# A hybrid diffusion-transformer layer on one core: the mixing projection's sums and operand splits go from GpSimd to VectorE, six of its weight blocks are split ahead, and a third early block's weights get tiles of their own

## The chip, the cores and the metric

One NeuronCore of a Trainium2 chip runs the whole layer in one launch. The metric is the device time in microseconds (us). The kernel before was timed three times: 2280.68, 2282.3 and 2285.83 us, median 2282.3. One execution was also recorded by the hardware profiler. TensorE is called PE in the profile (PEld is its weight load), VectorE is DVE, ScalarE is ACT, GpSimd is POOL, and SyncE is SP, whose queue issues every transfer here.

## The reference, cut to what matters

```python
mix = merge_branches(...)                 # ends in: return merged @ w_o
x_new = x + g1 * mix                      # 1024 tokens x 1024 channels
h2 = modulate(rmsnorm(x_new, norm2_g), sh2, sc2)   # * sc2 + sh2 per channel
x_new = x_new + g2 * swiglu(h2, w_ffn_in, w_ffn_out)

def swiglu(h, w_in, w_out):
    gu = h @ w_in                         # (1024, 1024) @ (1024, 5632)
    return (jax.nn.silu(gu[..., :D_FF]) * gu[..., D_FF:]) @ w_out
```

The change concerns the stretch from `merged @ w_o` to the first columns of `h @ w_in`.

## The kernel before, in words

All matrix products are made of three products of 128x512 outputs: an fp32 operand is split into a high part (`hi`, rounded by ScalarE to the type the PE reads) and a low part (`lo`, the fp32 value minus `hi`), and hi·hi, hi·lo and lo·hi are summed in PSUM (`mm3`, L203 to L205). So each operand block costs a cast on ScalarE and a subtraction on VectorE or GpSimd before the PE can use it.

Three stages touch the change. The stage ahead (the SSD output projection) ends with the gated sums `m1`, which are split into `mg[k][hf]` (L1229 to L1234). Beside it VectorE builds the second half of the adaLN vectors (L1194, L1196), and weights come through a pool of two raw tiles and three hi and lo tiles of 1024 columns each, filled by `wload` and `wsplit` (L198, L199).

The mixing projection (from L1271) goes over two halves `dh` of the output's columns. For each it needs eight weight blocks of 128x512, `wo[k]`. In the first half, blocks 0 to 2 come through that pool, each in one half of a 1024-column tile; blocks 3 to 7, and all eight of the second half, come through a pool `pe` that opens only with this stage: two raw tiles `wor`, nine tiles each of `woh` and `wol`, the low part on GpSimd (L1291). Then eight token blocks `t` follow: 24 matmuls into `em`, times the gate `g1bc` on VectorE (L1302), plus the residual `xr` (L1303, on GpSimd in the second half except for t = 7), a store to `s_xn`, and a sum of squares on ScalarE (L1305). In the second half VectorE and GpSimd make 1/rms (L1310 to L1312), VectorE scales (L1314), the PE transposes (L1317), and VectorE and ScalarE write the modulated `h2` in turn (L1324, L1321), four pieces of 128x128 for each group of transposes.

The feed-forward's input projection works with 2x2 blocks in seven products instead of eight (a Strassen scheme): its right-hand operands are quadrants of `h2` and their sums. `opB11` and `opB21` are the first two quadrants, complete after t = 3; they are split on ScalarE and GpSimd (`msplit(..., 1)`, L1263, L1264). Each of 22 steps `j` has two products that need only these (`f_first`), of 12 matmuls each, and five that need the rest. `f_first` for j = 0, 1 and 2 is placed ahead of the rest (L1372, L1374, L1400), so that the PE has work while the last token blocks are normalised. The weight block of j = 2 is the fourth in a ring `fraw` of three tiles, and the first tile of that ring is free when `w_combos(0)` has read it (L1407 to L1410 on VectorE). The other operands follow: `opB22` (L1264 again), `opT3`, `opT1`, `opT2` (`tsplit`, L1383, L1384, in a pool `mp2` of 24 tiles of 128x512) and `opT4`. Weight operands are split by `opsplit` (L1343, L1344); its argument `e` picks GpSimd (1) or VectorE (0) for the low part. In the first eleven steps each step also forms sums of output weights for the later stage (loads `fi`, sums on VectorE in L1437, stores `s_cw`).

The order on every engine is fixed when the kernel is built: a scheduler places the instructions of this part by its own cost model, and each engine then works through its list in order. A waiting instruction holds up everything behind it on its engine; SP's list does the same to transfers. Tiles of a pool that opens later lie where tiles of closed pools lay, and their first writer waits for the last reader of that memory, tile by tile.

Of the kernel before, what the change touches and what calls it, by code (L numbers as in the profile page):

```python
# [15 lines left out]
P = 128  # L16
# [125 lines left out]
def _build(nc, tc, h, o, hook, stop, es):  # L142
# [47 lines left out]
    def wload(src, cols=1024):  # L190
        raw = wp.tile([P, 1024], F32, name="wraw", bufs=NRAW)
        nc.sync.dma_start(out=raw[:, :cols], in_=src)
        return wsplit(raw, cols)
# [1074 lines left out]
    with pool("pe", "left") as pe, pool("ppe", "left", space=PSUM) as ppe:  # L1268
# [3 lines left out]
        for dh in range(2):  # L1272
# [8 lines left out]
            for k in range(KT):  # L1281
                if dh == 0 and k < NHL:
                    hi, lo = wload(h["wo"][k][:, ds_], 512)
                    wo.append((hi[:, :512], lo[:, :512]))
                    continue
                raw = pe.tile([P, 512], F32, name="wor", bufs=2)
                nc.sync.dma_start(out=raw, in_=h["wo"][k][:, ds_])
                hi = pe.tile([P, 512], F32R, name="woh", bufs=9)
                lo = pe.tile([P, 512], F32R, name="wol", bufs=9)
                nc.scalar.copy(out=hi, in_=raw)  # L1290
                nc.gpsimd.tensor_tensor(out=lo, in0=raw, in1=hi.bitcast(F32), op=ALU.subtract)  # L1291
                wo.append((hi, lo))
            for t in range(NT):
# [8 lines left out]
                nc.vector.tensor_tensor(out=x_, in0=ps, in1=g1bc[:, ds_], op=ALU.mult)  # L1302
                (nc.gpsimd if dh == 1 and t < NT - 1 else nc.vector).tensor_tensor(out=x_, in0=x_, in1=xr, op=ALU.add)  # L1303
                nc.sync.dma_start(out=s_xn[t][:, ds_], in_=x_)
# [8 lines left out]
                for q in range(2):  # L1313
# [4 lines left out]
                    for i in range(4):  # L1318
                        k = 4 * q + i
                        if i % 2:  # L1320
                            nc.scalar.activation(out=h2[hf][:, k, ts_], in_=tp[:, i, :], func=AF.Identity,  # L1321
                                                 scale=sc2[:, k:k + 1], bias=sh2[:, k:k + 1])
                        else:
                            nc.vector.tensor_scalar(out=h2[hf][:, k, ts_], in0=tp[:, i, :], scalar1=sc2[:, k:k + 1],  # L1324
                                                    scalar2=sh2[:, k:k + 1], op0=ALU.mult, op1=ALU.add)
                if t == 3:
                    for i in range(4):
                        opB11[i] = msplit(h2[0][:, i, :], 1)
                        opB21[i] = msplit(h2[0][:, 4 + i, :], 1)
                        nc.gpsimd.tensor_tensor(out=h2[0][:, 4 + i, :], in0=h2[0][:, 4 + i, :], in1=h2[0][:, i, :], op=ALU.subtract)  # L1330
# [33 lines left out]

    def f_first(j, pss=None, e=1):
        if (j, 0) not in fw:
            f_load(j, 0)
        rg = fw[(j, 0)]
        f12[j] = pss or [fq_ps() for _ in range(2)]
        product(f12[j][0], opsplit(rg[:, :512], e), opB11)  # L1370
        product(f12[j][1], opsplit(rg[:, 512:], 0), opB21)

    f_load(0, 0)
    f_load(0, 1)  # L1374
    f_first(0)
    ppf = es.enter_context(pool("ppf", "left", space=PSUM))
    f_first(1, [fq_ps(), fp_ps()])
    mp2 = fstack.enter_context(pool("mp2", "left"))

    def tsplit(src):  # L1380
# [17 lines left out]

    f_hold(1)
    f_first(2, [fp_ps(), fp_ps()])  # L1400
    f_hold(2)

# [13 lines left out]
    for i in range(4):  # L1416
        opB22[i] = msplit(qd(i)[3])
    product(p3_0, opsplit(wc[0][3], 1), opB22)
    for i in range(4):
# [12 lines left out]
    with pool("fb", "right") as fb, pool("fg", "right") as fg:  # L1432
# [25 lines left out]
        for j in range(NFF):  # L1458
# [13 lines left out]
            product(p7, opsplit(s3, 0), opT3)  # L1472
            product(p5, opsplit(s1, 1), opT1)
            product(p6, opsplit(w2, 0), opT2)
# [185 lines left out]
```

## Time and profile before

| | |
|---|---|
| median of three runs | 2282.3 us |
| profiled execution, device time | 2281.2 us |
| its span, first to last instruction | 2279.4 us |
| mean granted TensorE clock | 0.981 of full |
| PE busy | 2165.9 us (95%) |
| DVE busy | 1627.0 us (71%) |
| ACT busy | 991.4 us (43%) |
| POOL busy | 741.8 us (33%) |

The profiled execution lies 1.1 us under the median, and 1.8 us of it lie outside the span. Busy shares are means over stages with different limits; in this kernel the PE is busy nearly throughout, so the time that can go is where the PE stands still or runs at its lower clock. Times within the span are counted from its start. In the views of single instructions a row gives start, duration, engine, line, operation, output and inputs, count, and in brackets how long the engine stood idle before it and what ended that.

### The profile page before, as it was taken

Reading aid. Unit: us, or ns where it says so; the run is one execution under the profiler, and the core shown is the slowest. Engines: PE = TensorE matmul, PEld = TensorE weight load, DVE = VectorE, ACT = ScalarE, POOL = GpSimd, SP = SyncE. Lnnn points to the kernel's source line nnn. Section 1 sums busy time; section 2 is a strip of 40 time slices with the busy share of each in tenths; the row PEclk is TensorE's granted clock in tenths of the full one; section 3 lists DMA queues with packets and bytes.
Section 4 is the critical chain, followed back from the end, with each engine's and each line's share of the span. In section 5 each row is a group of like instructions: output and inputs, shape, how many; then the busy total and the mean of one; then the engine's idle time right before and its main releaser. Section 6 shows DMA issues by size and latency. Waiting matters only on the chain. (4 is left out here: it accounts for less than half of the span.)

```text
span 2279.4 us, 32757 instructions
## 1 busy us (share of the span) xinstructions
PE 2165.9 (95%) x11560; PEld 1813.0 (80%) x11560; DVE 1627.0 (71%) x2783; ACT 991.4 (43%) x2094; POOL 741.8 (33%) x610
## 2 busy tenths in 40 slices
PE   7999999999689999999999999999798999999997
PEld 1778888886588999999989887777576888887876
DVE  5878888888657777877736558826987566775678
ACT  4444444433345666767743212124422332334443
POOL 1532111110125555555521222135343333332222
PEclk9999999999799999999999999999899999999999
DMA  8122223432254555555454546551486224457755
GB/s 289 64 73 88 83 84 130 143 119 93 90 171 152 176 160 171 173 175 178 156 188 164 177 159 245 186 187 65 127 276 226 92 98 162 166 177 242 237 194 185
DMA packets 167101, 360.28 MB, mean 158 GB/s; under 512 B 17548, under 2 KB 57228, under 8 KB 166296
## 3 DMA queue, kind: packets, MB, share of 16 engines
q1 hardware_dynamic: 166936, 358.18, 47.0%
q8 instruction: 91, 1.49, 0.3%
q14 instruction: 74, 0.61, 0.1%
HBM read 267.34 MB, written 90.78 MB: 157 GB/s over the span
## 5 line engine op out<-in xcount | busy, mean ns | idle before, releaser
L199 POOL TENSOR_TENSOR wlo<-wraw,whi 128x1024 fp32r<-128x1024 f32 (+1 forms) x83 | 201.5, 2431 | 634.3 <-ACT whi L198 631.5
L198 ACT CAST whi<-wraw 128x1024 fp32r<-128x1024 f32 (+1 forms) x123 | 126.8, 1036 | 237.6 <-PE dm L210 84.2
L203 PE MATMUL fill<-whi,hhi 128*128 128x256 f32 x768 | 223.1, 292 | 7.1 <-DVE pad L576 5.8
L432 DVE SCALAR_TENSOR_TENSOR cv<-pad,vecs,cv 128x1282 f32<-128x1282 f32 (+1 forms) x128 | 213.8, 1709 | 7.8 <-ACT cv L429 7.4
L204 PE MATMUL fill<-wlo,hhi 128*128 128x256 f32 x768 | 218.1, 284 | 0.0
L205 PE MATMUL fill<-whi,hlo 128*128 128x256 f32 x768 | 217.4, 284 | 0.0
L874 ACT ACTIVATE abc<-abc,a_all 128x128 f32<-128x128 f32 x512 | 158.2, 392 | 88.4 <-DMA abc<-s_a 84.1
L203 PE MATMUL fp<-m,oph 128*128 128x512 f32 x452 | 181.3, 402 | 14.0 <-ACT oph L1343 10.4
L205 PE MATMUL fp<-m,opl 128*128 128x512 f32 x452 | 181.7, 403 | 8.0 <-DVE opl L1344 5.0
L204 PE MATMUL fp<-m,oph 128*128 128x512 f32 x452 | 181.2, 401 | 0.0
L495 PE MATMUL mm<-tq,whi 128*128 128x512 f32 x480 | 153.8, 401 | 1.4 <-ACT whi L198 1.4
L203 PEld LDWEIGHTS fill<-whi,hhi 128*128 128x128 f32 x768 | 145.8, 190 | 9.4 <-issue 6.2
L495 PE MATMUL mm<-hhi,whi 128*128 128x512 f32 x320 | 127.7, 400 | 22.4 <-DVE pad L570 22.4
L204 PEld LDWEIGHTS fill<-wlo,hhi 128*128 128x128 f32 x768 | 146.3, 191 | 0.7
L205 PEld LDWEIGHTS fill<-whi,hlo 128*128 128x128 f32 x768 | 146.0, 190 | 0.5
L495 PE MATMUL mm<-hlo,whi 128*128 128x512 f32 x320 | 127.1, 397 | 0.0
L495 PE MATMUL mm<-hhi,wlo 128*128 128x512 f32 x320 | 126.9, 397 | 0.0
L203 PEld LDWEIGHTS fp<-m,oph 128*128 128x128 f32 x452 | 86.5, 191 | 36.1 <-ACT oph L1343 11.7
L205 PEld LDWEIGHTS fp<-m,opl 128*128 128x128 f32 x452 | 86.3, 191 | 32.0 <-DVE opl L1344 7.6
L495 PEld LDWEIGHTS mm<-tq,whi 128*128 128x128 f32 x480 | 89.7, 189 | 22.7 <-ACT whi L198 2.5
L850 DVE SCALAR_TENSOR_TENSOR S<-S,decp,st 128x64 f32<-128x64 f32 x512 | 105.0, 273 | 0.0
L876 DVE COPY_PREDICATED abc<-misc,abc 128x512 f32<-128x512 int32 x64 | 52.3, 818 | 71.2 <-ACT abc L874 71.1
(408 smaller groups left out, 5919.0 us busy)
## 6 DMA issues: line engine op xcount, KB each, us to landing
abc<-s_a SPq DMA_DIRECT2D x64, 512.0 KB
fraw<-in_wfi SPq DMA_DIRECT2D x44, 512.0 KB
wraw<-in_wxbc SPq DMA_DIRECT2D x32, 512.0 KB
dx<-in_wada SPq DMA_DIRECT2D x32, 512.0 KB
wraw<-in_wzf SPq DMA_DIRECT2D x24, 512.0 KB
gt<-s_gate SPq DMA_DIRECT2D x24, 512.0 KB
fi<-in_wfo SPq DMA_DIRECT2D x22, 512.0 KB
s_cw<-fo SPq DMA_DIRECT2D x44, 256.0 KB
```

The lines of the kernel that those rows point to most:

```text
L198: nc.scalar.copy(out=hi[:, :cols], in_=raw[:, :cols])
L199: (eng or nc.gpsimd).tensor_tensor(out=lo[:, :cols], in0=raw[:, :cols], in1=hi[:, :cols].bitcast(F32), op=ALU.subtract)
L203: nc.tensor.matmul(ps, lhsT=a[0], rhs=b[0], start=start, stop=False)
L204: nc.tensor.matmul(ps, lhsT=a[0], rhs=b[1], start=False, stop=False)
L205: nc.tensor.matmul(ps, lhsT=a[1], rhs=b[0], start=False, stop=stop)
L432: nc.vector.scalar_tensor_tensor(out=v[:, :n], in0=pd[:, t:t + n], scalar=cwh[:, 5 * b + t:5 * b + t + 1], in1=v[:, :n], op0=ALU.mult, op1 ...
L495: nc.tensor.matmul(ps, lhsT=lhs[x], rhs=b[i][y], start=i == 0 and (x, y) == (0, 0), stop=i == 3 and (x, y) == (1, 0))
L850: nc.vector.scalar_tensor_tensor(out=sn[:, hd_], in0=S[-1][:, hd_], scalar=decp[:, i, d, 4 * g + j:4 * g + j + 1], in1=sv_[:, hd_], op0=AL ...
L874: nc.scalar.activation(out=abc[:, d, j, :], in_=abc[:, d, j, :], func=AF.Identity, scale=-1.0, bias=a_all[:, c, hd:hd + 1])
L876: nc.vector.copy_predicated(out=E, mask=tri_b.bitcast(mybir.dt.int32)[:, None, :].to_broadcast([P, HPG, P]), data=abc[:, 1])
```

## The change

In the first half of the projection six of the eight weight blocks now come through the older pool, two in each 1024-column tile (two transfers of 256 KB, one cast, one subtraction), and that subtraction is on VectorE. The low parts of the other two are on VectorE too. The residual additions of the second half are all on VectorE. For t below 7 ScalarE writes three of four pieces of `h2`, VectorE one. The low parts of `opB11` and `opB21`, those of the first products of j = 0, 1 and 2, and of two more weight operands of j = 0, are on VectorE. The weight block of j = 2 no longer waits for the ring: it is loaded into two of the 24 tiles of `mp2`.

```diff
-                if dh == 0 and k < NHL:
-                    hi, lo = wload(h["wo"][k][:, ds_], 512)
-                    wo.append((hi[:, :512], lo[:, :512]))
+                if dh == 0 and k < 2 * NHL:
+                    if k % 2 == 0:
+                        raw = wp.tile([P, 1024], F32, name="wraw", bufs=NRAW)
+                        for q in range(2):
+                            nc.sync.dma_start(out=raw[:, 512 * q:512 * q + 512], in_=h["wo"][k + q][:, ds_])
+                        hi, lo = wsplit(raw, eng=nc.vector)
+                        wo += [(hi[:, :512], lo[:, :512]), (hi[:, 512:], lo[:, 512:])]
                     continue
...
-                nc.gpsimd.tensor_tensor(out=lo, in0=raw, in1=hi.bitcast(F32), op=ALU.subtract)
+                (nc.gpsimd if dh else nc.vector).tensor_tensor(out=lo, in0=raw, in1=hi.bitcast(F32), op=ALU.subtract)
...
-                (nc.gpsimd if dh == 1 and t < NT - 1 else nc.vector).tensor_tensor(out=x_, in0=x_, in1=xr, op=ALU.add)
+                nc.vector.tensor_tensor(out=x_, in0=x_, in1=xr, op=ALU.add)
...
-                        if i % 2:
+                        if i % 2 or (i and t < NT - 1):
...
-                        opB11[i] = msplit(h2[0][:, i, :], 1)
-                        opB21[i] = msplit(h2[0][:, 4 + i, :], 1)
+                        opB11[i] = msplit(h2[0][:, i, :])
+                        opB21[i] = msplit(h2[0][:, 4 + i, :])
...
-    def f_first(j, pss=None, e=1):
-        if (j, 0) not in fw:
+    def f_first(j, pss=None, e=1, raw=None):
+        if (j, 0) not in fw and raw is None:
             f_load(j, 0)
-        rg = fw[(j, 0)]
+        rg = fw.get((j, 0))
         f12[j] = pss or [fq_ps() for _ in range(2)]
-        product(f12[j][0], opsplit(rg[:, :512], e), opB11)
-        product(f12[j][1], opsplit(rg[:, 512:], 0), opB21)
+        rg = (rg[:, :512], rg[:, 512:]) if raw is None else raw
+        product(f12[j][0], opsplit(rg[0], e), opB11)
+        product(f12[j][1], opsplit(rg[1], 0), opB21)
...
-    f_first(0)
+    f_first(0, e=0)
...
-    f_first(1, [fq_ps(), fp_ps()])
+    f_first(1, [fq_ps(), fp_ps()], e=0)
     mp2 = fstack.enter_context(pool("mp2", "left"))
+    early = [mp2.tile([P, 512], F32, name="m2", tag="m2", bufs=24) for _ in range(2)]
+    for q in range(2):
+        nc.sync.dma_start(out=early[q], in_=h["wfi"][2][:, 512 * q:512 * q + 512])
...
-    f_first(2, [fp_ps(), fp_ps()])
+    f_first(2, [fp_ps(), fp_ps()], e=0, raw=early)
...
-    product(p3_0, opsplit(wc[0][3], 1), opB22)
+    product(p3_0, opsplit(wc[0][3], 0), opB22)
...
-            product(p5, opsplit(s1, 1), opT1)
+            product(p5, opsplit(s1, int(j > 1)), opT1)
```

The built order shows what this moves. First the PE at the start of the mixing projection, before: the first matmuls that need a block of the later pool (`woh`, `wol`), behind 27 that need only blocks split ahead (`whi`, `wlo`; `m` is `mg`, `em_15072`, `em_15104` and `em_15136` are t = 0, 1 and 2).

```order
L205 MATMUL em_15136<-whi_15038,m_14544 128x512
L203 MATMUL em_15072<-woh_15044,m_14646 128x512
L203 MATMUL em_15104<-woh_15044,m_14646 128x512
L203 MATMUL em_15136<-woh_15044,m_14646 128x512
L204 MATMUL em_15072<-wol_15045,m_14646 128x512
```

The same place now, with t = 0, 1 and 2 in `em_15057`, `em_15089` and `em_15121`:

```order
L203 MATMUL em_15121<-whi_15041,m_14839 128x512
L203 MATMUL em_15057<-woh_15047,m_14921 128x512
L203 MATMUL em_15089<-woh_15047,m_14921 128x512
L204 MATMUL em_15121<-wlo_15042,m_14839 128x512
L205 MATMUL em_15121<-whi_15041,m_14840 128x512
L204 MATMUL em_15057<-wol_15048,m_14921 128x512
```

The first matmul with a late block moved from the 28th to the 53rd place of the stage.

Second, SP's list behind the last token block's store (`s_xn7`), before: the weight block of j = 2 is `fraw_15972`.

```order
L1304 DMA s_xn7_133<-xx1_15849 128x512 [waits DMAHW4_49,DVE_49]
L1356 DMA fraw_15972<-in_wfi 128x1024 [waits DMAHW5_49,DVE_49]
L1356 DMA fraw_16230<-in_wfi 128x1024 [waits DMAHW6_49,DVE_49]
L1442 DMA fi_16214<-in_wfo 128x1024 [waits DVE_49,DMAHW7_49,PE_49,Pool_49]
L1443 DMA fi_16215<-in_wfo 128x1024 [waits DMAHW0_49]
```

And now, where it is `m2_15948` and `m2_15949`:

```order
L1308 DMA s_xn7_133<-xx1_15834 128x512 [waits DMAHW4_49,DVE_49]
L1386 DMA m2_15948<-in_wfi 128x512 [waits DMAHW5_49]
L1386 DMA m2_15949<-in_wfi 128x512 [waits DMAHW6_49,PE_49]
L1360 DMA fraw_16217<-in_wfi 128x1024 [waits DMAHW7_49,DVE_49]
L1360 DMA fraw_16344<-in_wfi 128x1024 [waits DMAHW0_49,DVE_49]
L1450 DMA fi_16201<-in_wfo 128x1024 [waits DMAHW1_49,DVE_49,Pool_49]
```

Its load stands at the same place, but no longer waits for a VectorE instruction of its own; the two ring loads behind it are those of the next blocks.

Third, VectorE around the operands of j = 2 (`opl`) and of the first products that need the late quadrants (`m_16020` and on: `opB22`; `wt`: the four weight sums of j = 0), before:

```order
L1409 TENSOR_TENSOR wt_16013<-fraw_15883,wt_16011 128x512 [waits DVE_49]
L1410 TENSOR_TENSOR wt_16012<-fraw_15883,fraw_15885 128x512
L1335 TENSOR_TENSOR h20_15335<-h20_15335,h21_15336 128x4x128 [waits DVE_49]
L1264 TENSOR_TENSOR m_16028<-h21_15336,m_16027 128x512 [waits Activation_49]
L1264 TENSOR_TENSOR m_16032<-h21_15336,m_16031 128x512 [waits Activation_49]
...
L1425 TENSOR_TENSOR h21_15336<-h21_15336,h20_15335 128x512 x2
L1344 TENSOR_TENSOR opl_15991<-fraw_15972,oph_15990 128x512 [waits DMAHW5_49,Activation_49]
```

And now:

```order
L1264 TENSOR_TENSOR m_16011<-h21_15321,m_16010 128x512 [waits Activation_49]
L1348 TENSOR_TENSOR opl_15962<-m2_15948,oph_15961 128x512 [waits DMAHW5_49,Activation_49]
L1417 TENSOR_TENSOR wt_16000<-fraw_15868,wt_15998 128x512 [waits DVE_49]
L1418 TENSOR_TENSOR wt_15999<-fraw_15868,fraw_15870 128x512
L1348 TENSOR_TENSOR opl_15978<-m2_15949,oph_15977 128x512 [waits DMAHW6_49,Activation_49]
...
L1264 TENSOR_TENSOR m_16019<-h21_15321,m_16018 128x512 [waits Activation_49]
L1348 TENSOR_TENSOR opl_16023<-wt_16000,oph_16022 128x512 [waits Activation_49]
```

Both low parts of the block of j = 2 are now on VectorE, around the weight sums that the load used to wait for. From the gate multiplication of t = 7 to the last of the twelve low parts `m2` VectorE's list has 67 instructions before and 66 now: 47 before and 52 now are of 512 columns with two tensor inputs, 4 and 4 scalings of 512 columns, 14 and 8 pieces of `h2`, and two each of one column.

## Rows read from the trace of the kernel before

**Rows 1.** The page's first line: the span.

```profile
span 2279.4 us, 32757 instructions
```

**Rows 2.** Windows: stretch, length, busy time by engine (count), granted clock, DMA share, GB/s.

```profile
1442.30:1454.00 11.70, 11.70 (x56) 9.62 (x55) 11.13 (x16) 1.84 (x3) 2.45 (x2) 1.00 0.70 221
...
1491.10:1575.00 83.90, 83.90 (x382) 68.85 (x381) 31.83 (x65) 26.02 (x61) 29.58 (x26) 1.00 0.41 138
1575.00:1606.20 31.20, 16.23 (x81) 11.75 (x79) 27.70 (x47) 14.67 (x34) 16.98 (x15) 0.91 0.10 34
1606.20:1617.40 11.20, 8.17 (x18) 5.97 (x19) 10.90 (x14) 8.56 (x15) 9.22 (x3) 0.50 0.00 0
...
1680.00:1760.00 80.00, 72.22 (x292) 56.01 (x291) 62.69 (x82) 21.18 (x39) 26.77 (x18) 0.96 0.75 255
```

**Rows 3.** Timeline, PE, start of the mixing projection.

```profile
1484.15 0.39 PE L204 MATMUL em<-wlo,m 128*128 128x512 f32 x1
1484.38 0.39 PE L205 MATMUL em<-whi,m 128*128 128x512 f32 x1
1487.40 1.24 PE L203 MATMUL em<-woh,m 128*128 128x512 f32 x3 [2.63 <-ACT woh L1290]
...
1491.06 0.53 PE L203 MATMUL em<-woh,m 128*128 128x512 f32 x1
```

**Rows 4.** Timeline, PE, from the mixing projection to step j = 1.

```profile
1575.03 0.86 PE L203 MATMUL fq<-m,oph 128*128 128x512 f32 x3
...
1606.24 0.80 PE L203 MATMUL fp<-m,oph 128*128 128x512 f32 x1 [10.41 <-ACT oph L1343]
...
1612.16 0.80 PE L205 MATMUL fp<-m,opl 128*128 128x512 f32 x1 [2.99 <-POOL opl L1344]
...
1633.96 0.47 PE L203 MATMUL fp<-m,oph 128*128 128x512 f32 x1 [0.41 <-DVE fe L1485]
```

**Rows 5.** Timeline, SP and ACT: the weight block of j = 2.

```profile
1580.65 0.33 SPq L1304 DMA_DIRECT2D s_xn<-xx  x1
1601.98 19.13 SPq L1356 DMA_DIRECT2D fraw<-in_wfi  x2
...
1605.57 1.14 ACT L1343 CAST oph<-fraw 128x512 fp32r<-128x512 f32 x2 [6.91 <-DMA fraw<-in_wfi]
```

**Rows 6.** Timeline, DVE, from 1569 us to the last low part.

```profile
1569.71 0.88 DVE L1314 TENSOR_SCALAR xx<-xx,ems 128x512 f32<-128x512 f32 x2 [0.73 <-POOL ems L1312]
...
1578.06 0.68 DVE L1302 TENSOR_TENSOR xx<-em,g1bc 128x512 f32<-128x512 f32 x1
...
1581.07 2.90 DVE L1314 TENSOR_SCALAR xx<-xx,ems 128x512 f32<-128x512 f32 x2
...
1600.06 0.69 DVE L1333 TENSOR_TENSOR h<-h,h 128x512 f32<-128x512 f32 x1
1600.66 0.69 DVE L1409 TENSOR_TENSOR wt<-fraw,wt 128x512 f32<-128x512 f32 x1
...
1614.27 1.76 DVE L1264 TENSOR_TENSOR m<-h,m 128x512 fp32r<-128x512 f32 x1
...
1622.53 3.70 DVE L1384 TENSOR_TENSOR m<-h,m 128x512 fp32r<-128x512 f32 x6
```

**Rows 7.** Timeline, POOL: the low part for the first product of j = 2.

```profile
1606.27 5.84 POOL L1344 TENSOR_TENSOR opl<-fraw,oph 128x512 fp32r<-128x512 f32 x1 [14.29 <-ACT oph L1343]
```

**Rows 8.** Window of VectorE's 67 instructions, columns as in rows 2.

```profile
1578.06:1626.20 48.14, 30.14 (x120) 22.27 (x119) 45.08 (x70) 26.25 (x52) 23.14 (x15) 0.82 0.11 34
```

**Rows 9.** Groups by line and form, 1530 to 1600 us: busy, mean ns.

```profile
L1321 ACT ACTIVATE h<-etr,ada,sc 128x128 f32<-128x128 f32 x32 | 13.9, 457 | 24.5 <-DVE h L1324 24.4
L1324 DVE TENSOR_SCALAR h<-etr,sc,ada 128x128 f32<-128x128 f32 x32 | 12.6, 407 | 6.3 <-PE etr L1317 5.9
...
L1303 POOL TENSOR_TENSOR xx<-xx,xr 128x512 f32<-128x512 f32 x7 | 9.0, 1297 | 15.9 <-issue 9.5 <-DVE xx L1302 4.2 <-DMA xr<-in_xN 2.2
```

**Rows 10.** Line L199 over the whole kernel: ns min/median/max, first and last start.

```profile
L199 DVE TENSOR_TENSOR wlo<-wraw,whi x40: 1164/1220/3431, 116.3 to 620.8; 128x1024 fp32r<-128x1024 f32 x40
```

## The prediction, made before the changed kernel had run

> **What bounds the kernel now.** I read the stretches with their busy time first, then the PE's timeline at the two places where its share falls, and from each wait the engine that ended it. In the mixing projection the PE stands at 83.90 of 83.90 us with the clock at 1.00 [rows 2]: nothing that the change moves on other engines can shorten that part; it can only lengthen it. The time that can go lies at its two ends.
>
> At the start the PE runs out of split weights. Nine matmuls take from 1484.38 to 1491.06 us [rows 3]; at the full clock one follows the other after 0.23 us (1484.15 to 1484.38), which makes 2.1. So 4.6 us are lost: 2.63 waiting for the cast of the first late block, the rest in the matmuls behind it, which run at the lower clock or wait for GpSimd's low parts.
>
> At the end, from the first product of the feed-forward at 1575.03 to that of step j = 1 at 1633.96, 58.9 us pass [rows 4]. The PE's work in it is 11 products of 12 matmuls, 132 x 0.23 = 30.4 us, and some 3 us of transposes. The other 25 are waits and clock: busy 16.23 of the first 31.20 us, with one wait of 10.41 that ends with a cast, then 11.20 us at clock 0.50, half of full and so 1.2 GHz [rows 2, 4]. That cast waited for the weights of j = 2, whose load was issued at 1601.98 although SP's last entry ahead of it left at 1580.65; they were there 3.6 us later, at 1605.57 [rows 5]. The load waited for the ring tile that the weight sums read, which come to an end after 1601.26 in VectorE's list. VectorE is the bound here: from the gate multiplication of t = 7 at 1578.06 to its last low part at 1626.2 it is busy 45.08 of 48.14 us [rows 6, 8].
>
> **Part by part: the start.** Of the eight blocks six are now split before the stage begins. The PE has 52 matmuls ahead of the first that needs a late block, 25 more than before: 25 x 0.23 = 5.8 us of work behind 1484.38, so until about 1490.4. The first late block's matmul could start at 1487.40 [rows 3], and VectorE, which now takes its low part, needs 0.60 for one (1600.06 to 1600.66) [rows 6]. That covers it by some 2 us. The 4.6 us go, with bounds of 2.6 (the wait alone) and 4.6; I take 4.6, since without a stop there is no reason for the lower clock. Price: three low parts of 1024 columns on VectorE, 1.22 us each [rows 10], in the last blocks of the stage ahead, where it is busy 11.13 of 11.70 us [rows 2]. That could leave it up to 0.65 late in each, 2 in all; but part of the 11.13 was spent beside GpSimd's subtraction, and PE wants the last low part only some matmuls into the stage: 0 taken, 2 kept for the range. The three more transfers of 256 KB go where the transfer engines are busy 0.70.
>
> **In the middle.** The seven residual additions leave GpSimd (1.30 us each) for VectorE (0.60), 4.2 us of its time; the fourteen pieces of `h2` go to ScalarE at 0.46 us each against 0.41 [rows 6, 9]. VectorE is busy 31.83 of 83.90 us there, ScalarE 26.02 [rows 2]: both are hidden under the PE. They cost something only if the PE came to wait for a tile of `em`, of which there are three.
>
> **At the end.** The weights of j = 2 now follow the last token block's store at once. They need 3.6 us from issue to cast; the PE has 48 matmuls of j = 0 and 1 ahead, 11 us, and transposes. So they are hidden, and the wait of 10.41 goes as a wait for weights. What is late next is VectorE, and I work out the stretch by its list. From the gate multiplication of t = 7 to the last of the twelve low parts there are 47 instructions at 0.60, 14 pieces at 0.41, four scalings at 0.44 (0.88 for two, at 1569.71): 28.2 + 5.7 + 1.8 = 35.7 us. Measured busy are 45.1 [rows 8]: 9.4 us are instructions held up. The rows show by what: the same two scalings take 2.90 us instead of 0.88, one subtraction 1.76 instead of 0.69, while GpSimd works, and GpSimd's own subtraction took 5.84 instead of 1.30 beside a VectorE without pause [rows 6, 7, 9].
>
> The Trainium skill, SBUF — State Buffer, section Who interferes with whom, has a rule for it: a VectorE instruction with two SBUF inputs and a GpSimd instruction that reads SBUF exclude each other for their whole length. The trace agrees for subtractions beside subtractions (1.76 against 0.69). By the rule the 9.4 us go with GpSimd's work; without it they stay, which is a rival below.
>
> Now the list has 52 instructions at 0.60, 8 at 0.41, four at 0.44: 31.2 + 3.3 + 1.8 = 36.3 us. GpSimd keeps only four sums of 512 columns and the powers of one column. So VectorE does 0.6 us more and stands still 9.4 less. Its idle time of 3.1 us (48.14 - 45.08) I keep, bounds 1 and 8. Ahead of the list it started 3.0 us behind the PE's last matmul of t = 7 (first product of the feed-forward at 1575.03, gate multiplication at 1578.06); now the low parts of `opB11` and `opB21` stand there too, eight of them, 4.8 us, but mostly while t = 7's own matmuls (24 x 0.23 = 5.5) run: 2 taken, 0 and 5 the bounds. Behind the list the PE was 7.8 us late (1626.2 to 1633.96), because it had been slow; now it keeps up and has some 8 matmuls left, 2 us. Sum: 2 + 36.3 + 3.1 + 2 = 43.4 us instead of 58.9, 15.5 us less; the PE's own 33 us fit in.
>
> **What is given back.** From 1680 to 1760 us the PE does 72.22 of 80.00 us, while transfers keep their engines busy 0.75 at 255 GB/s [rows 2]. All that feeds this stretch (the loads, sums and stores of output weights) starts with the end of the same operands, so it moves forward with the products. One block of 512 KB leaves it, 2.1 us at that rate. The bounds are a gain of 2.1 and a loss of another 7.8 (what the PE does not work now, 80.00 - 72.22, a second time); I take a loss of 1.0.
>
> The sum: 4.6 + 15.5 - 1.0 = 19.1 us. The profiled execution took 2281.2 us, 1.8 beyond its span [rows 1]; it becomes 2262.1. It lies 1.1 under the median, so 2263.2 us is predicted against 2282.3.
>
> **The rivals.** *Transfers take it back.* The PE reaches j = 1 earlier than the sums of output weights allow, and the idle 7.8 us of the stretch from 1680 on double. For it: that stretch waits already; against it: both start together. 2263.2 + 6.8 = 2270.0.
>
> *More goes.* VectorE starts at once, idles 1 us instead of 3.1, and the lighter transfers give their 2.1: 2 + 2.1 + 3.1 = 7.2 us more, 2256.0.
>
> *The held-up time stays.* VectorE is 94% busy in its stretch. If its long instructions are not GpSimd's doing, the moved work comes on top and 9.4 us stay: 2272.6. Against it are the pairs of rows above. The Trainium skill, Perfetto Trace Analysis, section Optimizing Scalar/DVE Operations, advises the opposite of this change where VectorE is saturated, to hand work to ScalarE or even GpSimd, but doubts that this helps between those two; this is the result by the first half.
>
> *The block is not early.* Its two tiles lie where an earlier pool lay, and if the last reader of that memory is late, so is the load. The wait then shrinks only by what VectorE gains, about 3 of 10: some 7 us more, 2270. Against it: in SP's list only the previous entry of its queue and a PE instruction are waited for.
>
> *The slow clock, the one that ends slower.* If VectorE feeds the PE in small portions all through the end, the clock may stay at its lower level, as in the 11.20 us at 0.50. It decides from the point where 132 matmuls at twice the spacing, 0.46, take longer than VectorE's 43.4: they take 60.7 us. With the waits of 2.99 and 0.41 [rows 4], and the 3 of transposes at double length less what lies beside a wait, some 4, that is 68.1, 24.7 more: 2287.9. Against it: from 1575 to 1606 the clock was 0.91 although the PE worked half of the time.
>
> **How the numbers follow.** Forecast 0.49, with its own range of 2259 to 2267; transfers 0.20; more goes 0.14; held-up time 0.08; block late 0.05; slow clock 0.04. The bounds of the unsure terms (VectorE's idle time +5, its start +3, the stage ahead +2) and the rivals give 2253 to 2274. Faster by over 0.2% (about 4.6 us, what a measurement of this kernel can tell from no change) is every case but the slow clock and two rivals together: 0.93; no change 0.04, slower 0.03.
>
> **What would show it.** The wait of 2.63 at the first late block is gone and the projection starts at full clock throughout. The cast of j = 2 no longer waits for a transfer. VectorE's scalings of t = 7 take 0.88 for two, and its list ends some 40 us after t = 7's last matmul, not 51. The granted clock never falls to 0.50 between projection and step 1. It is wrong if waits for VectorE's low parts of over 10 us in all stand in the end stretch, or if the stretch 100 to 180 us after it holds more than 10 us of waits.

## The result, and the profile after

The changed kernel takes 2256.4 us in the median of four runs (2252.8 to 2259.8), against 2282.8 of the kernel before in the same measurement: a ratio of 0.9883, 95% interval 0.9864 to 0.9902. 26.4 us went, 19.1 were forecast (2263.2). The time lies inside the whole range of 2253 to 2274, but below the forecast's own range of 2259 to 2267.

The profiled execution of the changed kernel is the slowest of the four, and its span only 21.4 us shorter. So I cut both traces into stretches that hold the same work: from the first matmul of the projection (`em`) to the first product of the feed-forward, then by the number of the feed-forward's recorded matmuls, and at the end by the first matmul of the stage behind the last step (`fp<-oph`).

| stretch, us | before | changed | difference |
|---|---|---|---|
| all stages ahead of the projection | 1478.2 | 1483.1 | +4.9 |
| projection, to the first product | 96.8 | 93.1 | -3.7 |
| first product to the 133rd matmul | 57.9 | 43.9 | -14.0 |
| 133rd to 205th matmul | 19.0 | 17.3 | -1.6 |
| 205th matmul to the end of the 22 steps | 396.0 | 388.6 | -7.5 |
| the stage behind, to the end | 231.5 | 232.0 | +0.5 |

From the projection's start to the end the change saves 801.2 - 774.9 = 26.3 us, as much as the medians differ. The 4.9 us ahead of it are chance: over fourteen profiled executions of this study that start lies anywhere from 1474.6 to 1483.7. Six of these kernels don't have the blocks split ahead, which is all that the change puts into the stage there, and they scatter from 1475.0 to 1481.3 too; the last 200 matmuls ahead of the projection take 45.9 us in all fourteen.

The windows of the changed kernel that answer to [rows 2, 8] (stretch, length, then busy time and count of PE, its weight load, VectorE, ScalarE, GpSimd, then granted clock, DMA share, GB/s):

```profile
1442.30:1459.00 16.70, 16.70 (x77) 13.65 (x76) 15.79 (x22) 3.33 (x4) 2.40 (x1) 1.00 0.83 272
1483.10:1495.10 12.00, 12.00 (x52) 9.67 (x52) 7.09 (x11) 3.06 (x5) 0.00 (x0) 1.00 0.62 193
1483.10:1576.24 93.14, 93.14 (x426) 76.18 (x426) 48.41 (x85) 34.78 (x83) 18.27 (x17) 1.00 0.43 141
1576.24:1607.00 30.76, 25.60 (x117) 19.19 (x115) 27.43 (x54) 20.61 (x46) 2.75 (x3) 1.00 0.15 52
1607.00:1621.00 14.00, 11.09 (x43) 7.52 (x43) 13.69 (x24) 7.87 (x15) 1.29 (x1) 1.00 0.36 119
1579.45:1617.98 38.53, 30.60 (x131) 22.33 (x130) 36.01 (x69) 24.80 (x50) 1.08 (x2) 1.00 0.17 54
1637.00:1777.00 140.00, 137.10 (x580) 109.75 (x579) 112.05 (x149) 41.52 (x76) 56.72 (x36) 0.99 0.66 230
1680.00:1760.00 80.00, 77.10 (x323) 61.39 (x322) 59.96 (x82) 22.23 (x41) 30.14 (x21) 0.98 0.68 234
```

The PE stands nowhere in the whole projection (93.14 of 93.14), the stage ahead of it is not held up (16.70 of 16.70), and the clock is 1.00 where it was 0.50. VectorE's list of t = 7 is the sixth row: 36.01 us busy in 38.53, where it was 45.08 in 48.14.

The PE's waits in the end stretch, all that are over 0.2 us (start, duration, operation, in brackets the wait and what ended it):

```profile
1588.23 0.66 PE L1321 MATMUL etr<-misc,xx 128*128 128x128 f32 x4 [1.70 <-ACT h L1325]
1590.47 0.66 PE L1321 MATMUL etr<-misc,xx 128*128 128x128 f32 x4 [1.58 <-ACT h L1325]
1594.78 0.50 PE L203 MATMUL fp<-m,oph 128*128 128x512 f32 x1 [0.86 <-ACT h L1325]
1596.36 0.50 PE L205 MATMUL fp<-m,opl 128*128 128x512 f32 x1 [0.37 <-DVE opl L1348]
1607.80 0.50 PE L204 MATMUL fp<-m,oph 128*128 128x512 f32 x1 [1.44 <-DVE m L1392]
1610.12 0.50 PE L203 MATMUL fp<-m,oph 128*128 128x512 f32 x1 [0.89 <-ACT m L1391]
1613.82 0.50 PE L204 MATMUL fp<-m,oph 128*128 128x512 f32 x1 [1.07 <-DVE m L1392]
```

Together 7.9 us, in seven small waits, against waits of 10.41 and 2.99 at [rows 4] and four of 0.8 to 1.5 beside them, 17.9 in all. The clock stays at 1.00 through them. The weights of j = 2 leave SP's queue at 1582.84, the cast comes at 1593.23 and waits for nothing (SP's and ScalarE's timelines):

```profile
1582.84 0.93 SPq L1386 DMA_DIRECT2D m<-in_wfi  x2
```

```profile
1593.23 1.14 ACT L1347 CAST oph<-m 128x512 fp32r<-128x512 f32 x2
```

VectorE's scalings show what GpSimd's work does to them within the changed kernel alone. One pair runs beside one of GpSimd's four remaining subtractions (second fence), the last pair, of t = 7, beside nothing:

```profile
1572.26 1.60 DVE L1318 TENSOR_SCALAR xx<-xx,ems 128x512 f32<-128x512 f32 x2
...
1585.19 0.88 DVE L1318 TENSOR_SCALAR xx<-xx,ems 128x512 f32<-128x512 f32 x2
```

```profile
1571.49 1.68 POOL L1334 TENSOR_TENSOR h<-h 128x512 f32<-128x512 f32 x1 [0.28 <-DVE m L1264]
```

### The profile page after: what moved, and what is told of

The parts are those of the page before. It is cut to its first block, busy times and chain, and to the rows that moved or that the text cites. A ratio compares the mean times of both kernels' runs of the same rounds, so it can differ in the third digit from the quotient of the medians.

```text
span 2258.0 us, 32755 instructions
## 1 busy us (share of the span) xinstructions
PE 2160.5 (96%) x11560; PEld 1809.6 (80%) x11560; DVE 1632.6 (72%) x2795; ACT 993.1 (44%) x2105; POOL 702.7 (31%) x581
## 4 chain that ended last, share of the span: by engine, by line
PE 71%; DVE 12%; DMA 7%; ACT 4%; issue 4%; POOL 1%; SPq 1%; DVEq 0%; POOLq 0%; ACTq 0%
PE mm L495 14%; PE dm L210 8%; PE fp L204 6%; PE fp L205 5%; PE fp L203 5%; DMA abc<-s_a 3%; PE mm L497 3%; PE spq L210 2%; PE fill L203 2%; PE fill L205 2%; PE fill L204 2%; PE fq L204 2%; PE fq L205 2%; PE fq L203 2%; PE fill L210 2%
## 5 line engine op out<-in xcount | busy, mean ns | idle before, releaser
L199 POOL TENSOR_TENSOR wlo<-wraw,whi 128x1024 fp32r<-128x1024 f32 x80 | 199.3, 2495 | 596.9 <-ACT whi L198 581.5
L198 ACT CAST whi<-wraw 128x1024 fp32r<-128x1024 f32 x123 | 127.8, 1044 | 231.0 <-PE dm L210 81.3
```

The source lines that it names most:

```text
L198: nc.scalar.copy(out=hi[:, :cols], in_=raw[:, :cols])
L199: (eng or nc.gpsimd).tensor_tensor(out=lo[:, :cols], in0=raw[:, :cols], in1=hi[:, :cols].bitcast(F32), op=ALU.subtract)
```

## The experiments

Two theories stood against each other. The first is the forecast's: the gain is the sum of the projection's start and its end, and at the end both the late weights and GpSimd's work on operands cost time. The second, the order: any edit makes the scheduler place the eleven steps with output-weight sums anew, and their waits change with it. "Loss of the eleven steps" is the time from the 205th to the 781st matmul above 576 x 0.2333 = 134.4 us. These matmuls go from step 2 to the start of step 9. The 1068 behind them, to the end of the steps, take 249.2 us = 1068 x 0.2333 in every kernel but the paced ones (e7, e8, e10), so nothing is lost there.

The stretches of every kernel, in us (last columns: first projection matmul to the end; median; ratio to the runs of before on the same chip):

| kernel | projection | to 133rd | loss of eleven steps | 205th to end of steps | whole | median | ratio, 95% |
|---|---|---|---|---|---|---|---|
| before | 96.8 | 57.9 | 12.5 | 396.0 | 801.2 | | 1 |
| changed | 93.1 | 43.9 | 5.0 | 388.6 | 774.9 | 2256.4 | 0.9883 (0.9864 to 0.9902) |
| e1 | 93.1 | 55.2 | 9.5 | 393.1 | 790.0 | 2269.4 | 0.9961 (0.9946 to 0.9975) |
| e2 | 96.5 | 54.7 | 5.6 | 389.2 | 788.6 | 2271.6 | 0.9968 (0.9952 to 0.9983) |
| e3 | 96.5 | 54.8 | 9.3 | 392.9 | 792.5 | 2273.6 | 0.9975 (0.9964 to 0.9985) |
| e4 | 97.3 | 55.1 | 4.9 | 388.5 | 788.8 | 2271.0 | 0.9962 (0.9948 to 0.9977) |
| e5 | 93.1 | 50.2 | 3.6 | 387.2 | 778.6 | 2256.0 | 0.9900 (0.9885 to 0.9916) |
| e6 | 93.1 | 50.6 | 6.4 | 390.0 | 782.8 | 2265.1 | 0.9937 (0.9922 to 0.9951) |
| e7 | 93.1 | 43.8 | 0.0 | 386.4 | 772.6 | 2253.4 | 0.9886 (0.9872 to 0.9901) |
| e8 | 96.8 | 57.6 | 0.0 | 388.5 | 792.2 | 2273.5 | 0.9976 (0.9967 to 0.9985) |
| e9 | 93.1 | 44.1 | 5.2 | 388.8 | 774.6 | 2257.8 | 0.9892 (0.9872 to 0.9913) |
| e10 | 93.1 | 42.9 | 0.0 | 386.7 | 771.2 | 2252.9 | 0.9878 (0.9859 to 0.9897) |
| e11 | 93.1 | 46.0 | 5.2 | 388.7 | 777.9 | 2259.3 | 0.9904 (0.9886 to 0.9922) |
| e12 | 97.0 | 45.7 | 6.3 | 389.9 | 781.9 | 2259.9 | 0.9915 (0.9895 to 0.9936) |

### Each part alone

e1, the six blocks and the first half's low parts (line numbers here and below are those of the kernel that is edited):

```diff
-                if dh == 0 and k < NHL:
+                if dh == 0 and k < 2 * NHL:
...
-                nc.gpsimd.tensor_tensor(out=lo, in0=raw, in1=hi.bitcast(F32), op=ALU.subtract)
+                (nc.gpsimd if dh else nc.vector).tensor_tensor(out=lo, in0=raw, in1=hi.bitcast(F32), op=ALU.subtract)
```

> The kernel before with one part of the change: six weight blocks of the projection split ahead, low parts of the first half on VectorE. Theory (the forecast's terms add up): the wait of 2.63 us at the first late block is gone and the projection, 96.8 us from its first matmul to the first product of the feed-forward, takes 93.1 as in the changed kernel; nothing else changes: 2282.8 - 3.7 = 2279.1 us. Rival (order): every edit makes the scheduler place the eleven steps with output-weight sums anew; what these lose to waits (12.5 us before, 5.0 changed, between the 205th and the 781st matmul of the feed-forward) changes by several us with an edit that has nothing to do with them: 2272 to 2284.

The projection came as the theory said, 93.1 us. But the eleven steps, which the edit does not touch, lose 9.5 instead of 12.5 us, and the end, which it doesn't touch either, is 2.7 shorter: 2269.4, ten below the theory's 2279 and below the rival's 2272 too.

e2, the weights of j = 2 in two `m2` tiles:

```diff
+    early = [mp2.tile([P, 512], F32, name="m2", tag="m2", bufs=24) for _ in range(2)]
+    for q in range(2):
+        nc.sync.dma_start(out=early[q], in_=h["wfi"][2][:, 512 * q:512 * q + 512])
...
-    f_first(2, [fp_ps(), fp_ps()])
+    f_first(2, [fp_ps(), fp_ps()], raw=early)
```

> The kernel before with one part: the weights of j = 2 in two tiles of their own, their low part still on GpSimd. Theory (VectorE's list is the bound and GpSimd holds it up): the wait of 10.41 us for the cast goes, but VectorE's list keeps its 48 us; only the 6 us that the PE was late behind the list come back: about 2277. Rival (the weights were the matter): the first product to step j = 1 shrinks by the whole 10.4 and the clock's 4: about 2268. By the order rival the stretch behind it moves by several us on top, up or down.

The wait for the cast is gone, and the end keeps 54.7 of its 57.9 us, 3.2 less where the theory had 6 and its rival some 14: without the shorter list the early weights are worth little. The eleven steps lose 5.6, and so the total of 2271.6 lies under the theory's 2277.

e3, the low parts to VectorE:

```diff
-                        opB11[i] = msplit(h2[0][:, i, :], 1)
-                        opB21[i] = msplit(h2[0][:, 4 + i, :], 1)
+                        opB11[i] = msplit(h2[0][:, i, :])
+                        opB21[i] = msplit(h2[0][:, 4 + i, :])
...
-    f_first(0)
+    f_first(0, e=0)
...
-            product(p5, opsplit(s1, 1), opT1)
+            product(p5, opsplit(s1, int(j > 1)), opT1)
```

> The kernel before with one part: the low parts of opB11 and opB21, of the first products of j = 0, 1 and 2 and of two more operands of j = 0 on VectorE instead of GpSimd; weights of j = 2 still through the ring. Theory: VectorE's long instructions from 1606 us on (1.76 for 0.69) go and the wait of 2.99 for GpSimd's 5.84 us goes; the wait for the weights stays at some 8 to 10 us: 5 us faster, about 2278. Rival (held-up time is not GpSimd's doing): VectorE has eight more subtractions of 0.6 and the list ends later: 2283 to 2287.

GpSimd's wait is gone and that for the weights is down to 5.04 us, but the PE now waits 6.1 us for ScalarE's pieces of `h2` at the transposes; 3.1 us off the end. The rival (slower) has fallen. The eleven steps lose 9.3, and 2273.6 is under the theory's 2278. (The edit of `opT1`'s product also covers j = 1, ahead of the 205th matmul, and not j = 0 alone.)

e4, residual additions on VectorE and three of four pieces on ScalarE:

```diff
-                (nc.gpsimd if dh == 1 and t < NT - 1 else nc.vector).tensor_tensor(out=x_, in0=x_, in1=xr, op=ALU.add)
+                nc.vector.tensor_tensor(out=x_, in0=x_, in1=xr, op=ALU.add)
...
-                        if i % 2:
+                        if i % 2 or (i and t < NT - 1):
```

> The kernel before with one part: residual additions of the second half on VectorE, three of four pieces of h2 on ScalarE for t below 7. Theory: hidden under the PE except in the last token blocks, where it takes 2 us off VectorE's list, while the wait for the weights of j = 2 stays: 2280 to 2283. Rival (order): the eleven steps lose 5 us instead of 12.5, or more than 12.5, though nothing in them is edited: below 2277 or above 2286.

2271.0: under the rival's bound of 2277. The end gives 2.8 us (waits of 9.54 and 2.96 stay), the eleven steps 7.6. Each of the four edits made the kernel 6 to 9 us faster by its ratio (as the start ahead of the projection scatters, the column "whole" is the cleaner one: 8.7 to 12.6). In all four between 3.0 and 7.6 us come from steps whose operations none of them edits, as the order rival has it in kind; e2 only takes one load out of their ring. The traces show that the order did change: the list of transfers on SP between the 205th and the 781st matmul is another in each of these four kernels, in the kernel before and in the changed one. The kernel before has one profile, but its 24 runs beside these four bear its longer time out (median 2280.5).

### The change without a part

e5, the weights of j = 2 through the ring again:

```diff
-    f_first(2, [fp_ps(), fp_ps()], e=0, raw=early)
+    f_first(2, [fp_ps(), fp_ps()], e=0)
```

> The changed kernel without one part: the weights of j = 2 come through the ring again, everything else as changed. Theory (both the early weights and the shorter VectorE list are needed for the end): the wait for the cast is back, some 5 us as with the low parts alone, and the stretch from the first product to the 133rd matmul takes 50 to 53 us instead of 43.9: 2263 to 2266. Rival (the early block is the whole end): 55 us as in each part alone: about 2268. Both plus or minus what another order of the eleven steps does (their loss 5 to 10 us).

The end came as the theory said, 50.2 us, with the wait back (PE's timeline):

```profile
1593.23 0.79 PE L203 MATMUL fp<-m,oph 128*128 128x512 f32 x1 [6.23 <-ACT oph L1347]
```

The early block is thus worth 6.3 us there, once the rest is changed. Its total still missed the theory's: in this kernel's order the eleven steps lose only 3.6 us and the stretch ahead of them is 0.5 shorter, so that its 2256.0 can't be told from the changed kernel by the times; from the projection's start to the end it is 3.7 us longer.

e6, the low parts on GpSimd again (the edit of e3 undone):

```diff
-                        opB11[i] = msplit(h2[0][:, i, :])
-                        opB21[i] = msplit(h2[0][:, 4 + i, :])
+                        opB11[i] = msplit(h2[0][:, i, :], 1)
+                        opB21[i] = msplit(h2[0][:, 4 + i, :], 1)
...
-    f_first(2, [fp_ps(), fp_ps()], e=0, raw=early)
+    f_first(2, [fp_ps(), fp_ps()], raw=early)
```

> The changed kernel without one part: the low parts of opB11, opB21, of the first products of j = 0, 1 and 2 and of two operands of j = 0 are on GpSimd again. Theory (shared time of GpSimd and VectorE): the wait of 2.7 us for GpSimd's low part is back and VectorE has instructions of 1.7 us again; the first product to the 133rd matmul takes 50 to 53 us instead of 43.9: 2262 to 2266. Rival (GpSimd's work is hidden once the weights are early): 44 to 46 us: 2256 to 2258.

50.6 us, the theory's, and 2265.1. The size was right, the way was sharper than expected. The PE's wait, GpSimd's row behind it, and the window of that row (columns as above):

```profile
1606.75 0.79 PE L205 MATMUL fp<-m,opl 128*128 128x512 f32 x1 [10.87 <-POOL opl L1348]
```

```profile
1594.82 11.88 POOL L1348 TENSOR_TENSOR opl<-m,oph 128x512 fp32r<-128x512 f32 x1 [9.49 <-ACT oph L1347]
1606.66 3.41 POOL L1348 TENSOR_TENSOR opl<-wt,oph 128x512 fp32r<-128x512 f32 x2
```

```profile
1594.82:1606.70 11.88, 1.03 (x4) 0.30 (x2) 11.88 (x20) 7.43 (x14) 11.88 (x2) 0.70 0.14 44
```

One subtraction of 128x512 takes GpSimd 11.88 us, nine times its 1.30, while VectorE runs through its list without a pause (11.88 of 11.88 us); VectorE itself is slowed only at its end and behind it, beside GpSimd's next two. The mean clock is 0.70 in this window.

e11, residual additions and pieces of `h2` as before (e4 undone):

```diff
-                nc.vector.tensor_tensor(out=x_, in0=x_, in1=xr, op=ALU.add)
+                (nc.gpsimd if dh == 1 and t < NT - 1 else nc.vector).tensor_tensor(out=x_, in0=x_, in1=xr, op=ALU.add)
...
-                        if i % 2 or (i and t < NT - 1):
+                        if i % 2:
```

> The changed kernel without one part: the residual additions of the second half on GpSimd again, pieces of h2 half and half between ScalarE and VectorE. Theory (these shorten VectorE's list in the last token blocks by six pieces of 0.41 and keep GpSimd off its port): the first product to the 133rd matmul takes 47 to 49 us instead of 43.9: 2259 to 2262. Rival (hidden under the PE, as the forecast had it): 44 us, 2256. Both plus or minus what another order of the eleven steps does.

46.0 us, between the theory's 47 and the rival's 44: this part is worth 2.1 us at the end and 1.1 between the 133rd and the 205th matmul.

e12, the blocks not split ahead (e1 undone):

```diff
-                if dh == 0 and k < 2 * NHL:
+                if dh == 0 and k < NHL:
```

> The changed kernel without one part: the six weight blocks split ahead. VectorE's order in the eleven steps is word for word that of the changed kernel. Theory: the projection takes 96.8 us instead of 93.1, and every other stretch is as in the changed kernel (43.9, loss 5.0): 2260. Rival (the early start is taken back at the end): the projection 96.8, the end shorter by as much: 2256.

The projection takes 97.0 us, as it should; the rival (shorter end) has fallen, the end is 1.8 longer. That 2259.9 is the theory's 2260 is luck: it had added only the 3.7. From the projection's start to the end e12 is 7.2 us longer than e9, while the medians of the two, on the same chip, differ by only 2.1: the stretch ahead of the projection scatters by more than the part is worth. Between the 205th and the 781st matmul every engine and SP work through the same list as in the changed kernel, and yet 6.3 us are lost in place of 5.0 (5.2 in e9).

### The eleven steps

What the order costs is seen in the kernel before, at the step around 1735 us. VectorE's sum waits for a store, and the operation that the PE needs stands behind it (VectorE's timeline, then the PE's):

```profile
1730.85 0.69 DVE L1437 TENSOR_TENSOR fo<-fi 128x512 f32<-128x512 f32 x1 [1.49 <-DMA fi<-in_wfo]
1735.08 0.69 DVE L1437 TENSOR_TENSOR fo<-fi,fo 128x512 f32<-128x512 f32 x1 [3.53 <-DMA s_cw<-fo]
1735.68 0.68 DVE L1485 TENSOR_TENSOR fe<-fe,fp 128x512 f32<-128x512 f32 x1
```

```profile
1736.51 0.47 PE L203 MATMUL fp<-m,oph 128*128 128x512 f32 x1 [2.29 <-DVE fe L1485]
```

e7 gives the changed kernel, and e8 the kernel before, one ring for the sums and the step's own results, so that a step's sums can't run ahead:

```diff
-            t = [fg.tile([P, 512], F32, name="fo", bufs=5) for _ in range(4)]
+            t = [fb.tile([P, 512], F32, name="fe", bufs=13) for _ in range(4)]
...
-            return fb.tile([P, 512], F32, name="fe", bufs=8)
+            return fb.tile([P, 512], F32, name="fe", bufs=13)
```

> The changed kernel with one edit more: the output-weight sums take their tiles from the ring of the step's own results (13 tiles instead of 8 and 5 apart), so a step's sums can't run ahead of it; four sums stand in each of the eleven steps, behind the step's own work. Theory (the eleven steps lose time to low parts that stand behind sums waiting for loads, and to loads in a bunch): the 5.0 us that they lose between the 205th and the 781st matmul fall to 1 or less: about 2252. Rival (transfers are the limit whatever the order): 5 us stay, and what is pushed later makes new waits: 2256 to 2262.

> The kernel before with that same single edit on the ring of the sums, none of the change. Theory: the loss of 12.5 us in the eleven steps falls to 1 or 2, while the end of the projection keeps its 55 to 58 us: 2269 to 2271. Rival: the loss is the transfers' and stays near 10: 2278 to 2283.

In both the loss between the 205th and the 781st matmul is gone. The windows of 140 us from the 205th matmul on, first of the kernel before, then of e8 (columns as above):

```profile
1652.00:1792.00 140.00, 132.22 (x548) 104.33 (x549) 109.02 (x142) 40.10 (x72) 52.83 (x34) 0.98 0.66 224
```

```profile
1649.00:1789.00 140.00, 140.00 (x602) 112.68 (x601) 101.03 (x139) 42.32 (x77) 53.49 (x36) 1.00 0.53 187
```

The groups of the sums on VectorE show what changed, 1640 to 1780 us, first of the kernel before, then of e8 (busy, mean ns, idle before them and what ended it):

```profile
L1437 DVE TENSOR_TENSOR fo<-fi 128x512 f32<-128x512 f32 x20 | 21.4, 1072 | 8.0 <-DMA fi<-in_wfo 8.0
L1437 DVE TENSOR_TENSOR fo<-fi,fo 128x512 f32<-128x512 f32 x20 | 18.2, 908 | 6.9 <-DMA s_cw<-fo 3.5 <-issue 1.7 <-DVE fo L1437 0.9
```

```profile
L1437 DVE TENSOR_TENSOR fe<-fi 128x512 f32<-128x512 f32 x15 | 19.0, 1266 | 0.0
L1437 DVE TENSOR_TENSOR fe<-fi,fe 128x512 f32<-128x512 f32 x16 | 13.4, 839 | 0.0
```

40 sums in that time, with 14.9 us of idle time ahead of them, 11.5 of it put down to transfers, become 31 with none. Part is given back in the steps behind: from the 781st matmul to the last step e8 takes 254.1 us and e7 252.0, where it is 249.2 without pacing. So pacing saves 7.6 of 12.5 us in the steps of the kernel before, where 2273.5 comes out, above the theory's 2271, and 2.2 of 5.0 in those of the changed one. The rival (10 us stay whatever the order) has fallen. But the paced order also moves less in this stretch (187 GB/s in place of 224), so the place of the sums in VectorE's list and the bunching of their transfers aren't told apart.

e9 and e10 are the changed kernel and e7 again, without an edit, on one chip:

> The changed kernel unaltered, to see which of its stretches repeat. Theory (the order, not chance, sets the waits): projection 93.1 us, first product to the 133rd matmul 43.9, loss of the eleven steps 5.0, each within 1 us; what differs between runs lies ahead of the projection, in code that the change doesn't touch. Rival (chance in the transfers): the loss of the eleven steps comes out anywhere between 4 and 12.

> The kernel with paced sums again, beside the changed kernel on the same chip. Theory: it is faster than the changed kernel by the part of the 5.0 us that isn't lost again in the later steps (stretch from the 205th matmul to the last step 386.4 us against 388.6), so by 2 to 3 us: about 2253.5 against 2256. Rival: the two can't be told apart.

From the projection to the last step every stretch repeats within 0.3 us (e9) and 1 us (e10), the loss of 5.0 as 5.2: the waits of an order are in the main not chance. Pacing gives 2252.9 against 2257.8 us, and 771.2 and 772.6 against 774.6 and 774.9 us in the profiles. The intervals of the ratios overlap, so by the times alone it isn't settled; by the stretches it is 2 to 4 us faster. It beats the kernel before by 1.2% (0.9878, 0.9859 to 0.9897).

## Why the prediction was right, and where not

*The start: right.* The wait of 2.63 us and the low clock behind it are gone, and the first late block comes after 52 matmuls at full clock. The projection is 3.7 us shorter rather than 4.6, because the changed order also puts 40 transposes into it instead of 32, work that the end no longer has: (93.1 - 384 x 0.2333) / 40 makes an estimate of 0.09 us for each, so some 0.7 for the eight. The windows of the transposes alone, before and after (PE first):

```profile
1478.20:1575.03 96.83, 4.14 (x32) 3.73 (x32) 6.16 (x16) 6.54 (x16) 0.98 0.44 144
```

```profile
1483.10:1576.24 93.14, 5.82 (x40) 4.90 (x41) 3.98 (x10) 10.92 (x30) 1.00 0.43 141
```

*The end: right in its mechanism, 1.5 us too high.* 15.5 us were worked out, 14.0 came. 1.0 of that is the end point taken in the trace of before: the 133rd matmul, the first of step j = 1, stands at 1632.92, and 1633.96 is the third. The sum for the stretch came within 0.5, 43.9 for 43.4. VectorE's list was put at 36.3 us busy and 3.1 idle, and took 36.0 and 2.5; it started 3.2 us behind the projection instead of 2, and the PE needed 2.1 behind it. The clock stayed at 1.00. The early weights and the low parts are worth about twice as much beside the other parts (leaving them out costs 6.3 and 6.7 us) as alone (3.2 and 3.1). Of the 3 us alone not all need be their own, for e1, which edits nothing in the end stretch, takes 2.7 off it as well, and a kernel with these two parts alone was not run. The forecast counted the shared time as VectorE's; in e6 the PE's wait is for GpSimd: 10.87 us at one of its instructions.

*In the middle: half wrong.* Costed at nothing, the residual additions and pieces of `h2` are worth 2 to 3 us (e11), though the PE's time in the projection is the same 93.1 without them: the end is longer.

*What is given back: wrong, in sign and beyond its bounds.* This is the step that failed. A loss of 1.0 us was taken, with bounds of a gain of 2.1 and a loss of 7.8; the stretch from the 205th matmul to the last step gained 7.5, and the 72 matmuls ahead of it 1.6. The working assumed that the steps' feed only moves forward with the products. But the order of the eleven steps is the scheduler's, and it was placed anew with each edit: four edits of other operations moved their loss from 12.5 to between 4.9 and 9.5 us, and one that paces the sums made it zero, with and without the change, though 2.8 and 4.9 us of that came back behind it. So 3.7 + 14.0 + 1.6 + 7.5 less 0.5 behind them is 26.3 in place of 19.1. The rival *more goes* named 2256.0, nearly the time measured, but mostly by a VectorE that starts at once and idles 1 us; it started 3.2 us late and idled 2.5. Its number came by luck, and so did the time's place inside the whole range: the forecast's own range misses it. *Transfers take it back*, *the block is not early*, *held-up time stays* and *the slow clock* are each excluded by a row above.

Open is which place in the order of before cost its 7 us over the changed kernel: the start of the steps and the order moved together, and only the sums' running ahead was taken away by itself. e12, with the changed kernel's order on every engine, lost 6.3 instead of 5.0, so the order is not all.

## What to carry to other kernels

When a scheduler orders the work, an edit in one stage can change the order in the next, as most did here, and a forecast that only sums the edited stage leaves that out: put the stages behind it in the range by what they lose to waits now. Work that can run ahead of its turn (sums that depend on loads alone) puts its waits in front of work that is due; a shared ring that ties it to the step took 7.6 of 12.5 us away in the kernel before, and 2.2 of 5.0 in the changed one. And compare stretches that hold the same matmuls: they repeat within a microsecond where the start of the projection scatters by nine.

## What the runs showed of the hardware

A GpSimd subtraction beside a VectorE without pause is held up for nearly all of that run: 11.88 us for 1.30 in e6, and two that take 6.31 us together in e2. The price shows on whichever engine has its operand on the path, and it is much larger on GpSimd's side than on VectorE's (1.76 for 0.69 in [rows 6]). The two GpSimd subtractions of e2:

```profile
1599.29 6.31 POOL L1344 TENSOR_TENSOR opl<-wt,oph 128x512 fp32r<-128x512 f32 x2 [5.82 <-ACT oph L1343]
```

The rule that the prediction weighed (the Trainium skill, SBUF — State Buffer, section Who interferes with whom) lets the first of the two hold the shared access for its whole instruction. The rows agree that one of the two is held, and add how long that can last: GpSimd got no turn either between eighteen VectorE instructions in e6, all with both inputs in SBUF.

The rows also show what ended it. VectorE's list in e6 at the end of GpSimd's 11.88 us, which is at 1606.70:

```profile
1605.49 0.68 DVE L1404 TENSOR_TENSOR hold<-hold,fp 128x512 f32<-128x512 f32 x1
1606.09 1.16 DVE L1392 TENSOR_TENSOR m<-h,m 128x512 fp32r<-128x512 f32 x1
1607.17 1.76 DVE L1264 TENSOR_TENSOR m<-h,m 128x512 fp32r<-128x512 f32 x1
```

The `hold` addition is the first in that run with an input in PSUM (`fp`); GpSimd's subtraction ends 1.21 us after its start, about as long as it takes alone, and the VectorE instruction behind it is the first that is longer. From 1400 us on the traces have six GpSimd subtractions of more than 3.6 us (one in e6, two in e2, one each in before, e4 and e8). Each ends 1.1 to 1.2 us after the first VectorE instruction with an input in PSUM, or after VectorE's first pause. So the 5.84 us of [rows 7] were not quite beside a VectorE without pause: GpSimd's turn came with one of 0.30 us. Once it has a turn, the two take turns: GpSimd's next two in e6 take 3.41 us together, beside VectorE's two of 1.76.
